# Ordering the residual stream's transposes ahead of other side work in a hybrid decoder step on one Trainium2 core

## The chip, the core and the metric

The kernel runs on one core of a Trainium2 chip. The metric is the time of one execution in device microseconds, taken as the median of several runs. The core's engines work side by side, each through its own list of instructions in a fixed order: TensorE (PE in the profile), VectorE (DVE), ScalarE (ACT), GpSimd (POOL) and SyncE (SP), whose list holds nearly all the DMA transfers. An instruction waits at the head of its engine's list until what it needs is there, and everything behind it on that engine waits too.

## The reference

One decoder layer is computed for two groups of requests that share the weights: a prompt of 1024 tokens, and 8 samples of 8 tokens with 512 past tokens each in a paged cache (1088 tokens in all, model width 1024).

```
h = rmsnorm(x, norm_mix)
q, k, v, qi, ki, wi, bg, cg, xc, ga, gb = split(h @ w_in)      # rotary on q, k, qi, ki
score = sum_heads(wi * relu(qi . ki)); idx = top_k(score, 256)  # per query, causal
o_a = softmax(q . k[idx]) @ v[idx]
conv_o, conv_new = short_conv(cg * xc, conv_prev, conv_w)       # width 3
x = x + (sigmoid(ga) * o_a + sigmoid(gb) * bg * conv_o) @ w_out
x = x + (silu(g) * u) @ w_down                                  # g, u from rmsnorm(x)
x = x + (p @ w_ple) * sigmoid(rmsnorm(x) @ w_ple_gate)
y = rmsnorm(x, norm_final)
```

The results are y for both groups, the new keys, values and indexer keys, and the last two inputs of the convolution. Everything is in float32; a product is made as three matmuls of a high and a low part of each operand (hi*hi, lo*hi, hi*lo).

## The kernel before, in words

All activations are kept transposed: 128 features on the partitions, tokens along the free axis. The tokens are worked in three chunks of 384, 384 and 320 (`CH`). The input projection is a main line of work: `run_group` makes, for one block of 128 output features and one chunk, 24 matmuls of line 191 (`pj<-h_..,w..`, 8 slices of the width times three products), and goes on to the next chunk and block. The weights come as `wraw`; ACT rounds them to `wh` and POOL subtracts to get `wl` (line 151).

Everything else hangs beside that line as a side stream, a Python generator that emits a few instructions and then says what it needs next: `phase_a` (loads x, normalises it, transposes it to h, chunk by chunk), the indexer's scores, a search of the top 256 by counting on DVE, attention, and so on. The class `Weaver` decides while the program is built whose instructions come next. It keeps a clock of its own for each engine from fixed costs; at each step it takes the first side stream, in the order of its list, whose next instruction would be ready for TensorE now, else the main line, else whatever will be ready first (lines 270 to 310). What it decides is the order in the finished program: at run time each engine goes through its list as it stands.

The streams matter here in three ways. First, `x_keep` (lines 792 to 815) makes a transposed copy of the unnormalised x for the later additions: for each of nine tiles of 128 tokens (the last has 64) it loads x again from memory (SP, 512 KB), makes 8 transposes on TensorE (`pt<-ident,x`, line 198, four into each of two banks `pt`), two copies out by ACT (`xT<-pt`) and one store by SP to the scratch `x_scr`. The tile `xT` comes from a ring called L2, and a load of the next tile of x goes into SP's list behind the store of the one before. The ring `pt` has two banks, shared with `phase_a`, the rotary code's transposes (`pt<-ident,rt`) and attention. Second, `state_in` loads the convolution's state (`sraw`) and makes 8 small transposes of it. Third, the searches run on DVE and attention runs behind them: it needs the outcome of the searches for its masks, and uses TensorE (`at`, `po`), DVE (`mx`, `ptl`) and ACT in turn.

`main` runs the first group `g_first`, then issues four small loads (`c_tri`, `smask`, `sdelta`, `ptab`), and only then starts the streams `state_in`, `x_keep` and the scores, in that order.

Of the kernel before, what the change touches and what calls it, by code (L numbers as in the profile page):

```python
# [105 lines left out]
class Weaver:  # L106
# [162 lines left out]
    def run(self, main):  # L269
        m = Stream(main)  # L270
        LAG_D = 1.5
        while True:
            while self.active < self.max_active and self.queue:
                s = Stream(self.queue.popleft())
                s.t, s.queued = self.T["pe"], True
                self.active += 1
                self.sides.append(s)
            if m.done and not (self.sides or self.queue or self.pending):
                break
            pe = self.T["pe"]  # L280
            self._flush(pe)
            if m.done and not (self.sides or self.queue or self.pending):
                break
            pick = None
            for s in self.sides:
                if not self._hard(s):
                    continue
                if s.kind == "dve":
                    ok = self.T["dve"] <= pe + LAG_D and self._ready(s) <= pe + LAG_D
                elif s.kind == "soon":  # L290
                    ok = self._ready(s) <= max(pe + 0.2, self.T["dve"])
                else:
                    ok = self._ready(s) <= pe + s.ahead and self.T["dve"] <= pe + s.lag and self.T["act"] <= pe + s.lag
                if ok:
                    pick = s
                    break
            if pick is None and not m.done and self._hard(m) and self._ready(m, 3.0) <= pe + 0.3:
                pick = m
            if pick is None:
                best = min((w for w, _ in self.pending), default=None)  # L300
                for s in self.sides + ([] if m.done else [m]):
                    if self._hard(s):
                        r = self._ready(s, 3.0 if s is m else 0.0)
                        r = max(r, self.T["dve"] - LAG_D) if s.kind == "dve" else r
                        if best is None or r < best:
                            best, pick = r, s
                assert best is not None, "no stream can go on"
                self.log.append((max(pe, best) - pe, pick, m)) if hasattr(self, "log") else None
                self.T["pe"] = max(pe, best)
                if pick is None:  # L310
                    continue
            self._step(pick)
            m.t = 0.0
# [3 lines left out]
def hybrid_decoder_step(ctx, tc, I, O):  # L317
# [340 lines left out]
    def x_rows(i):  # L658
        return x_p[i * P:(i + 1) * P, :] if i < 8 else x_s
# [33 lines left out]
    def phase_a():  # L693
        spot = {i: s_all[:, (i - 5) * DM:(i - 4) * DM] for i in range(5, 9)}
        junk = [tM([P, DM], BF, name="junk_a"), tM([P, DM], BF, name="junk_b")]
        xt, tx = {}, {}

        def fetch(c):
            for i, m in tok_tiles(c):
                xt[i] = spot[i] if i in spot else tp_([P, DM], name="x")  # L700
                tx[i] = W.dma(xt[i][:m], x_rows(i))
        yield {"p": 5}
        fetch(0)
        wts.load()
        wts.load()
        fetch(1)
        load_tabs(64)
        sqrt_table()
        ps = psum("po")
        for _ in range(12):  # L710
            W.mm(ps[:, :384], ones, warm, 384, True, True, f32=True)
        W.give("po")
        ev_s = [Ev() for _ in CH]

        def stats(c):

            tl = tok_tiles(c)
            w = len(tl)
            ss = tpool.tile([P, 16], F32, tag="ss", name="ss", bufs=2)
            nc.vector.memset(ss, 1.0)  # L720
            te = t0 = W.cur.t
            for j, (i, m) in enumerate(tl):
                W.cur.t = max(t0, tx[i])
                yield None
                if j == 1:
                    W.go("dve", 1.2)
                    nc.vector.tensor_tensor_reduce(out=junk[1][:m], in0=xt[i][:m], in1=xt[i][:m], scale=1.0, scalar=0.0,
                                                   op0=OP.mult, op1=OP.add, accum_out=ss[:m, j:j + 1])
                else:
                    W.act(junk[0][:m], xt[i][:m], AF.Square, DM, accum_out=ss[:m, j:j + 1])  # L730
                te = max(te, W.cur.t)
            W.cur.t = te
            yield None
            W.ts(ss[:, 4:4 + w], ss[:, 0:w], 1.0 / DM, EPS, OP.mult, OP.add, w)
            W.act(ss[:, 8:8 + w], ss[:, 4:4 + w], AF.Sqrt, w)
            if c == 0:
                t0 = W.cur.t
                wts.pump(True, 1)
                wts.pump(True, 1)
                W.cur.t = t0  # L740
            yield None
            rsqrt(ss[:, 8:8 + w], ss[:, 4:4 + w], ss[:, 12:12 + w], w)
            t0 = te = W.cur.t
            for j, (i, m) in enumerate(tl):
                W.cur.t = t0
                x, r = xt[i][:m], ss[:m, 8 + j:9 + j]
                if j == 0:
                    W.act(x, x, AF.Copy, DM, scale=r)
                elif j == 1 or c == 0:
                    W.ts(x, x, r, None, OP.mult, None, DM)  # L750
                else:
                    W.go("pool", 0.12 + DM * 0.00105)
                    nc.gpsimd.tensor_scalar(x, x, r, 1.0, op0=OP.mult, op1=OP.mult)
                te = max(te, W.cur.t)
            ev_s[c].t = te

        for _ in stats(0):
            pass
        t0 = W.cur.t
        W._flush(1e9)  # L760
        fetch(2)
        ps = psum("pt")
        W.tr(ps[:, 0:56], gtmp[:56, :], ident[:56, :56])
        W.act(gvec, ps[:, 0:56], AF.Copy, 56)
        W.give("pt")
        W.give("S", 2)
        W.cur.t = t0
        for c, (c0, n) in enumerate(CH):
            tl = tok_tiles(c)
            yield ev_s[c]  # L770
            te = W.cur.t
            th = []
            for k in range(KT):
                W.cur.t = te
                tag = "at" if k % 2 else "pt"
                yield {tag: 1}
                ps = psum(tag)
                for j, (i, m) in enumerate(tl):
                    W.tr(ps[:, j * P:j * P + m], xt[i][:m, k * P:(k + 1) * P], ident[:m, :m])
                hs = H["hi"][:, k, c0:c0 + n]  # L780
                W.act(hs, ps[:, :n], AF.Copy, n, scale=g_mix(k))
                W.stt(H["lo"][:, k, c0:c0 + n], ps[:, :n], g_mix(k), hs.bitcast(F32), OP.mult, OP.subtract, n)
                W.give(tag)
                th.append(W.cur.t)
            W.give("p", sum(1 for i, m in tl if i not in spot))
            ev_h[c].t = max(th[1], th[-1] - 3.5)
            if c + 1 < len(CH):
                W.cur.t = 0.0
                yield from stats(c + 1)
        W.give("M", 2)  # L790

    def x_keep():

        for i in range(9):
            m = P if i < 8 else NS
            yield {"p": 1, "L2": 1}
            x, o = tp_([P, DM], name="x"), L2([P, KT, P], name="xT")
            W.load(x[:m], x_rows(i))
            for hf in range(2):
                yield {"pt": 1}  # L800
                ps = psum("pt")
                for k in range(4):
                    W.tr(ps[:, k * P:k * P + m], x[:m, (4 * hf + k) * P:(4 * hf + k + 1) * P], ident[:m, :m])
                t0 = W.cur.t
                W.act(o[:, 4 * hf:4 * hf + 4, :m], ps.rearrange("p (k t) -> p k t", t=P)[:, :, :m], AF.Copy, 512)
                W.give("pt")
                te, W.cur.t = W.cur.t, t0
            W.give("p")
            W.cur.t = te

            def store(i=i, m=m, o=o):
                W.store(x_scr[:, :, i * P:i * P + m], o[:, :, :m])
                W.give("L2")
            W.later(store)
# [1596 lines left out]
            yield from (run_rows if kind == "rows" else run_pair)(*a)  # L2411
    def main():
        wts.pump()
        yield from run_group(g_first)
        W.dma(tri, I["c_tri"])
        W.dma(smask, I["c_smask"])
        W.dma(sdelta, I["c_sdelta"])
        W.dma(ptab, I["page_table"].rearrange("b n -> (b n)").unsqueeze(0))
        W.spawn(state_in(), front=False)
        W.spawn(x_keep(), front=False)  # L2420
        W.spawn(score_stream([2, 3, 4, 5, 6, 7]), front=False)
        W.spawn(samp_idx(), front=False)
        W.spawn(search([2, 3, 4, 5], "a"), kind="dve", front=False)
# [81 lines left out]
```

## Time and profile before

| | |
|---|---|
| median of three runs | 1964.89 us |
| the runs | 3744.03, 1963.82, 1964.89 us |
| the profiled execution | 1964.83 us, of which the span is 1963.1 us |
| TensorE busy | 1911.7 us, 97% |
| VectorE busy | 1278.8 us, 65% |
| ScalarE / GpSimd busy | 701.7 / 750.5 us |
| mean granted clock of TensorE | 0.992 |

The profile shows one execution. The span runs from its first instruction to its last; the time lies 1.7 us above it. A busy figure is the time in which an engine had an instruction in work. The rest is waiting, and the profile puts each wait down to the last thing that ended it.

### The profile page before, as it was taken

Reading aid. Unit: us, or ns where it says so; the run is one execution under the profiler, and the core shown is the slowest. Engines: PE = TensorE matmul, PEld = TensorE weight load, DVE = VectorE, ACT = ScalarE, POOL = GpSimd, SP = SyncE. Lnnn points to the kernel's source line nnn. Section 1 sums busy time; section 2 is a strip of 40 time slices with the busy share of each in tenths; the row PEclk is TensorE's granted clock in tenths of the full one; section 3 lists DMA queues with packets and bytes.
Section 4 is the critical chain, followed back from the end, with each engine's and each line's share of the span. In section 5 each row is a group of like instructions: output and inputs, shape, how many; then the busy total and the mean of one; then the engine's idle time right before and its main releaser. Section 6 shows DMA issues by size and latency. Waiting matters only on the chain.

```text
span 1963.1 us, 35813 instructions
## 1 busy us (share of the span) xinstructions
PE 1911.7 (97%) x13337; PEld 1852.5 (94%) x13337; DVE 1278.8 (65%) x2691; ACT 701.7 (36%) x1403; POOL 750.5 (38%) x662
## 2 busy tenths in 40 slices
PE   8999989999999999999999899999999999999998
PEld 5998889998999989989999899999999999999998
DVE  6646999999999975214338885665665643314754
ACT  5355433213443235323334542322322322213543
POOL 2543455223322233114444342322322454424883
PEclk9999999999999999999999999999999999999999
DMA  4565335222322222546443432222222443212343
GB/s 154 170 190 151 99 105 145 54 56 66 85 65 52 63 74 54 154 126 198 126 146 121 145 101 76 77 83 70 79 83 66 139 150 99 89 47 85 105 135 118
DMA packets 293688, 206.27 MB, mean 105 GB/s; under 512 B 28912, under 2 KB 273192, under 8 KB 293514
## 3 DMA queue, kind: packets, MB, share of 16 engines
q1 hardware_dynamic: 293190, 203.63, 35.1%
q8 instruction: 105, 1.72, 0.4%
q14 instruction: 69, 0.57, 0.1%
q10 hardware_dynamic: 324, 0.36, 0.1%
HBM read 152.61 MB, written 51.31 MB: 104 GB/s over the span
## 4 chain that ended last, share of the span: by engine, by line
PE 81%; DVE 9%; issue 3%; DMA 3%; POOL 2%; SPq 1%; ACT 0%; DVEq 0%; POOLq 0%; ACTq 0%
PE pj L155 44%; PE pj L191 26%; PE at L187 4%; PE po L187 3%; PE pt L198 3%; DVE junk L1235 2%; SPq L164 1%; DVE ru L136 1%; POOL wl L151 1%; DVE cum L1271 1%; PE at L198 1%; DMA wraw<-in_w_in 1%; DMA qh<-qh_scr 0%; DVE scores L140 0%; DVE cv L140 0%
## 5 line engine op out<-in xcount | busy, mean ns | idle before, releaser
L151 POOL TENSOR_TENSOR wl<-wraw,wh 128x512 fp32r<-128x512 f32 (+2 forms) x234 | 302.4, 1295 | 660.2 <-ACT wh L132 636.5
L191 PE MATMUL pj<-h_hi,wh 128*128 128x384 f32 (+2 forms) x1197 | 404.9, 338 | 0.6 <-DVE ru L136 0.3
L191 PE MATMUL pj<-h_hi,wl 128*128 128x384 f32 (+2 forms) x1197 | 394.0, 329 | 0.7 <-POOL wl L151 0.7
L191 PE MATMUL pj<-h_lo,wh 128*128 128x384 f32 (+2 forms) x1197 | 393.6, 329 | 0.0
L132 ACT ACTIVATE wh<-wraw 128x512 fp32r<-128x512 f32 (+2 forms) x234 | 142.3, 611 | 295.8 <-PE pj L155 136.7
L191 PEld LDWEIGHTS pj<-h_hi,wh 128*128 128x128 f32 (+1 forms) x1197 | 226.4, 189 | 10.7 <-issue 6.3
L191 PEld LDWEIGHTS pj<-h_lo,wh 128*128 128x128 f32 (+1 forms) x1197 | 226.3, 189 | 2.8
L191 PEld LDWEIGHTS pj<-h_hi,wl 128*128 128x128 f32 (+1 forms) x1197 | 225.7, 189 | 1.8 <-POOL wl L151 1.1
L155 PE MATMUL pj<-f_hi,wl 128*128 128x272 f32 x704 | 204.3, 290 | 5.5 <-DVE wl L136 5.5
L155 PE MATMUL pj<-f_hi,whl 128*128 128x272 f32 x1056 | 206.0, 288 | 0.0
L155 PE MATMUL pj<-f_hi,wh 128*128 128x272 f32 x704 | 204.0, 290 | 0.3 <-DVE q_lo L136 0.2
L155 PE MATMUL pj<-f_lo,wh 128*128 128x272 f32 x704 | 203.3, 289 | 0.2 <-DVE f_lo L136 0.2
L136 DVE TENSOR_TENSOR x<-pj,x 128x272 f32<-128x272 f32 (+2 forms) x144 | 67.0, 469 | 173.4 <-PE pj L155 170.0
L155 PE MATMUL pj<-m_hi,wh 128*128 128x272 f32 (+2 forms) x586 | 176.1, 300 | 1.2 <-DVE x L136 0.7
L155 PE MATMUL pj<-m_hi,wl 128*128 128x272 f32 (+2 forms) x586 | 175.7, 300 | 0.0
L155 PE MATMUL pj<-m_lo,wh 128*128 128x272 f32 (+2 forms) x586 | 175.5, 300 | 0.0
L155 PEld LDWEIGHTS pj<-f_hi,whl 128*128 128x128 f32 x1056 | 168.7, 189 | 0.0
L155 PE MATMUL pj<-f_lo,whl 128*128 128x272 f32 x528 | 152.3, 288 | 0.0
L155 PEld LDWEIGHTS pj<-f_hi,wl 128*128 128x128 f32 x704 | 133.6, 190 | 5.9 <-DVE wl L136 5.9
L155 PEld LDWEIGHTS pj<-f_hi,wh 128*128 128x128 f32 x704 | 133.4, 189 | 0.6 <-issue 0.6
L155 PEld LDWEIGHTS pj<-f_lo,wh 128*128 128x128 f32 x704 | 133.3, 189 | 0.4 <-DVE f_lo L136 0.4
L151 POOL TENSOR_TENSOR whl<-wraw,whl 128x512 fp32r<-128x512 f32 x68 | 94.2, 1388 | 74.0 <-ACT whl L132 72.0
(376 smaller groups left out, 4488.1 us busy)
## 6 DMA issues: line engine op xcount, KB each, us to landing
wraw<-in_w_in SPq DMA_DIRECT2D x112, 256.0 KB
wraw<-in_w_gate_up SPq DMA_DIRECT2D x96, 256.0 KB
wraw<-in_w_down SPq DMA_DIRECT2D x40, 256.0 KB
wraw<-in_w_out SPq DMA_DIRECT2D x32, 256.0 KB
wraw<-in_w_ple_gate SPq DMA_DIRECT2D x32, 256.0 KB
x<-in_x_prompt SPq DMA_DIRECT2D x13, 512.0 KB
m_scr<-q_lo SPq DMA_DIRECT2D x19, 272.0 KB
q_lo<-m_scr SPq DMA_DIRECT2D x18, 272.0 KB
```

Of the source, the lines that this page charges most:

```text
L132: self.nc.scalar.activation(out, in_, func, **kw)
L136: self.nc.vector.tensor_tensor(out, a, b, op=op)
L151: self.nc.gpsimd.tensor_tensor(out, a, b, op=op)
L155: self.nc.tensor.matmul(ps, l, r, start=start, stop=stop)
L164: self.nc.sync.dma_start(out, in_)
L187: self.nc.tensor.matmul(ps, l, r, start=start, stop=stop)
L191: self.nc.tensor.matmul(ps, l, r, start=start, stop=stop)
L198: self.nc.tensor.transpose(ps, in_, ident)
L1235: nc.vector.tensor_scalar(junk[:m, :L], score[q], cand[:m, i:i + 1].bitcast(F32), None, op0=op, op1=OP.add, accum_out=cnt[:m, i:i + 1])
L1271: nc.vector.tensor_tensor_scan(cum, eq, eq, 0.0 if last is None else last, op0=OP.add, op1=OP.bypass)
```

## The change

`x_keep` is started ahead of `run_group(g_first)`, so it stands in the list before `state_in` and the scores. It begins once the loads of the last chunk of x have been issued (`ev_x2`). Until `g_first` is through, its transposes are of a kind `fill`: the Weaver takes them only where no side stream and not the main line has an instruction ready. From then on they are of the ordinary kind, and the stream is asked first among those that were started in `main`.

```diff
@@ class Weaver, run @@
             for s in self.sides:
                 if not self._hard(s):
                     continue
+                if s.kind == "fill":
+                    continue
...
                 pick = m
+            if pick is None:
+                pick = next((s for s in self.sides if s.kind == "fill" and self._hard(s) and self._ready(s) <= pe + 0.2), None)
             if pick is None:
                 best = min((w for w, _ in self.pending), default=None)
@@ phase_a @@
         fetch(2)
+        ev_x2.t = W.cur.t
@@ x_keep @@
+    keep, ev_x2 = ["fill"], Ev()
+
     def x_keep():
 
+        yield ev_x2
         for i in range(9):
             m = P if i < 8 else NS
+            W.cur.kind = "pe"
             yield {"p": 1, "L2": 1}
             x, o = tp_([P, DM], name="x"), L2([P, KT, P], name="xT")
             W.load(x[:m], x_rows(i))
+            W.cur.kind = keep[0]
             for hf in range(2):
@@ main @@
         wts.pump()
+        W.spawn(x_keep(), front=False)
         yield from run_group(g_first)
...
         W.spawn(state_in(), front=False)
-        W.spawn(x_keep(), front=False)
+        keep[0] = "pe"
+        for s in W.sides:
+            s.kind = "pe" if s.kind == "fill" else s.kind
         W.spawn(score_stream([2, 3, 4, 5, 6, 7]), front=False)
```

The instructions are the same ones; their order differs. The change moves the nine groups of 8 transposes forward in TensorE's list, from instructions 325 to 938 of some 13,100 to instructions 161 to 724, and it moves the 8 transposes of `sraw` back from 275 to 838. The first place is TensorE at the start of chunk 3's transposes of the normalised x (`scores` is where that chunk's x lies). A piece of the difference:

```order
 L191 MATMUL pj<-h_lox,wh 128x384
 L191 MATMUL pj<-h_hix,wl 128x384
+L198 MATMUL pt<-ident,x 128x128 x8
 L198 MATMUL pt<-ident,scores 128x128 x2
 L198 MATMUL pt<-ident,scores 128x64
```

The first tile of `x_keep` now stands between the last matmul of a chunk and the transposes of the next one. The second tile stands at the end of `g_first`, ahead of the first 128x384 matmul of the next block. The third stands 30 matmuls further: 24, three transposes of `rt`, and 6 more.

The second place is SP at that third tile, in the loads behind `g_first`. Before:

```order
L164 DMA ptab_95<-in_page_table 1x32
L164 DMA sraw_644<-in_state_conv 16x1024
L164 DMA wraw_688<-in_w_in 128x4x128
L164 DMA qi_scr_61<-ru_622 128x256
L164 DMA qi_scr_61<-rt_621 128x256
```

And now:

```order
L164 DMA ptab_95<-in_page_table 1x32
L164 DMA x_scr_67<-xT_526 1024x1x128
L164 DMA x_714<-in_x_prompt 128x1024
L164 DMA wraw_717<-in_w_in 128x4x128
L164 DMA qi_scr_61<-ru_641 128x256
L164 DMA qi_scr_61<-rt_640 128x256
```

The load of the third tile of x, and a load of weights behind it, now stand behind the store of the second tile's `xT`. On ACT the two copies that make this `xT` stand right behind a group of three `wh<-wraw 128x512`, ahead of `ki_hi<-rt 64x256`; no `xT` stood there before.

The third place is TensorE at the end of attention, where the last of its outputs `ob` is transposed (its instruction 5119 before, 5053 now). Before:

```order
L191 MATMUL pj_10323<-h1_lo_98,wh_9941 128x384
L191 MATMUL pj_10323<-h1_hi_96,wl_9942 128x384
L198 MATMUL pt_10359<-ident_85,ob_10351 128x128
L191 MATMUL pj_10323<-h1_hi_96,wh_9966 128x384
L191 MATMUL pj_10323<-h1_lo_98,wh_9966 128x384
```

And now:

```order
L191 MATMUL pj_10220<-h1_lo_98,wh_9872 128x384
L191 MATMUL pj_10220<-h1_hi_96,wl_9873 128x384
L198 MATMUL pt_10272<-ident_85,ob_10264 128x128
L191 MATMUL pj_10220<-h1_hi_96,wh_9872 128x384
L191 MATMUL pj_10220<-h1_lo_98,wh_9872 128x384
```

Of the projection's matmuls of line 191, 612 stood behind that transpose before and 678 do now: 66 more. On DVE, whose list holds the same work ahead of the last of attention's `ptl<-pt,pth` but for one instruction, nothing of that size has moved. Of TensorE's list the first 161 and the last 8,000 or so instructions are in the same order in both.

## Rows read from the trace of the kernel before

**Rows 1.** The page's head and its busy times (engine, us, share, instructions).

```profile
span 1963.1 us, 35813 instructions
PE 1911.7 (97%) x13337; PEld 1852.5 (94%) x13337; DVE 1278.8 (65%) x2691; ACT 701.7 (36%) x1403; POOL 750.5 (38%) x662
```

**Rows 2.** Windows by stage: stretch, length, busy time (count) of each engine, clock, DMA.

```profile
0.00:195.00 195.00, 182.81 (x1050) 158.98 (x1051) 116.84 (x216) 96.38 (x210) 78.88 (x80) 0.96 0.57 167
195.00:700.00 505.00, 488.58 (x3012) 471.08 (x3010) 479.83 (x1201) 164.89 (x355) 180.48 (x194) 0.99 0.28 78
```

**Rows 3.** Timeline around 44 us: start, duration, engine, instruction, [idle before, releaser].

```profile
43.63 1.15 ACT L132 ACTIVATE scores<-scores,ss 128x1024 f32<-128x1024 f32 x1 [1.04 <-DVE ss L136]
44.83 0.86 PE L198 MATMUL pt<-ident,scores 128*128 128x128 f32 x3 [1.65 <-ACT scores L132]
```

**Rows 4.** Timeline of 61 to 82 us, all engines.

```profile
64.75 0.63 ACT L132 ACTIVATE wh<-wraw 128x512 fp32r<-128x512 f32 x1 [3.76 <-DMA wraw<-in_w_in]
66.08 0.47 SPq L164 DMA_DIRECT2D ptab<-in_page_table  x1
66.55 0.33 PE L191 MATMUL pj<-h_hi,wh 128*128 128x384 f32 x1
67.04 0.39 SPq L164 DMA_DIRECT2D wraw<-in_w_in  x1
68.64 0.67 PE L198 MATMUL pt<-ident,sraw 16*128 16x16 f32 x8 [0.89 <-DMA sraw<-in_state_conv]
73.14 0.42 SPq L164 DMA_DIRECT2D x<-in_x_prompt  x1
73.23 0.63 ACT L132 ACTIVATE wh<-wraw 128x512 fp32r<-128x512 f32 x1 [1.43 <-PE pj L191]
77.27 1.06 PE L198 MATMUL pt<-ident,x 128*128 128x128 f32 x8 [1.09 <-DMA x<-in_x_prompt]
78.09 0.42 PE L191 MATMUL pj<-h_hi,wh 128*128 128x384 f32 x1
77.93 1.09 ACT L132 ACTIVATE xT<-pt 128x512 f32<-128x512 f32 x2 [2.25 <-PE pt L198]
79.04 0.57 SPq L164 DMA_DIRECT2D x_scr<-xT  x1
79.67 1.80 SPq L164 DMA_DIRECT2D x<-in_x_prompt  x1
```

**Rows 5.** Windows around chunk 3's transposes, and at 77 us (columns as in Rows 2).

```profile
46.10:51.70 5.60, 5.60 (x19) 2.87 (x19) 4.59 (x9) 4.45 (x10) 1.81 (x3) 0.50 0.00 0
51.80:56.20 4.40, 4.40 (x20) 3.94 (x20) 2.46 (x5) 1.49 (x4) 0.81 (x2) 0.50 0.27 93
56.40:61.00 4.60, 4.60 (x33) 4.57 (x32) 1.73 (x5) 1.81 (x4) 1.05 (x2) 1.00 0.34 78
77.20:82.00 4.80, 4.73 (x30) 4.76 (x31) 0.86 (x2) 1.92 (x4) 2.74 (x4) 1.00 0.85 237
```

**Rows 6.** Timeline at 1128 us, TensorE.

```profile
1127.78 0.40 PE L155 MATMUL pj<-f_hi,wl 128*128 128x272 f32 x1 [4.34 <-DVE wl L136]
```

**Rows 7.** Windows behind that wait (columns as in Rows 2).

```profile
1128.00:1131.50 3.50, 3.50 (x17) 3.50 (x17) 3.46 (x6) 2.13 (x5) 1.42 (x1) 0.51 0.24 66
1131.50:1135.00 3.50, 3.50 (x30) 3.50 (x29) 2.48 (x6) 1.29 (x3) 0.03 (x1) 1.00 0.30 88
```

**Rows 8.** Waits of DVE in 195 to 700 us.

```profile
DVE u L136 <- PE pj L191: 3.0, 3, 2.2
DVE cv L136 <- PE pj L191: 2.1, 3, 1.3
DVE p L1304 <- PE at L187: 1.2, 3, 0.7
DVE rt L136 <- PE pj L191: 1.1, 1, 1.1
```

## The prediction

> **What bounds the kernel now.** I read the page's busy times first. TensorE is busy 1911.7 of 1963.1 us [rows 1], so the kernel can gain little by moving work: all of TensorE's waits together are 1963.1 - 1911.7 = 51 us, and a change that only reorders can take some of them away or add to them. Next come the windows by stage [rows 2]. In the first 195 us TensorE is busy 182.81 us, and the reader should see that DVE has slack there (116.84 us). Between 195 and 700 us that is gone: DVE is busy 479.83 of 505 us beside TensorE's 488.58. In this stretch two engines are near full, and either may set the pace. Then the timeline, for the three waits that lie where the change works. TensorE stands still for 1.65 us ahead of chunk 3's transposes, until ACT has scaled x [rows 3]; for 0.89 us until `sraw` has landed, and for 1.09 us until the first tile of x for `x_keep` has landed [rows 4]. Last come the granted clock in windows of a few us [rows 5, 7]: it tells what a wait costs beyond its own length.
>
> **The change, part by part.** No instruction is added, so every term is a wait or the clock.
>
> *First tile.* Its 8 transposes go into the 1.65 us wait. Eight take 0.82 us (from 77.27 to the next matmul at 78.09 [rows 4]). But they take both banks `pt`, and chunk 3's first transposes need one back. The copies out stand on ACT behind the scaling, which ends at 43.63 + 1.15 = 44.78 [rows 3]; two copies take 1.09 us [rows 4], so the first bank is free at about 45.33 instead of the start at 44.83. The wait shrinks by 0.82 and grows by 0.50: **-0.32 us**. The ends: -0.82 if the bank costs nothing, +0.3 if chunk 3's own copies, now behind both of these on ACT, are late throughout.
>
> *The two other waits.* The wait for `sraw` goes, since its transposes come over 500 instructions later and its load is then long landed: **-0.89**. The wait of 1.09 goes, since the first tile's load now stands on SP right behind chunk 3's own, which ACT is scaling by then: **-1.09**.
>
> *Third tile.* Here a new wait appears, and this is the step I trust most. The ring L2 gives out one tile at a time at this point, so the third load stands on SP behind the second tile's store, and that behind ACT's two copies. On ACT the copies stand behind the third `wh`, which itself waits for its weights and runs from 64.75 to 65.38; two copies more end at 66.47. SP is through with `ptab` at 66.55, the store takes 0.57, so the load is issued at 67.12. From issue to the first transpose a tile took 77.27 - 73.14 = 4.13 us: 71.25. TensorE gets there after six matmuls of a new chunk, where the seventh started at 66.55 before, and now 0.50 later for the first tile and 0.82 for the second: 67.87. All of this is [rows 4]. The wait is 71.25 - 67.87 = **+3.4 us**. The ends are 1.1 (the wait that the same load left before) and 5.5 (issued over 1.80 us, as the row at 79.67, and landing as much later). Behind that load on SP is a load of weights, moved back from 67.04 by some 2 us; what it feeds starts at 73.23 and waited for TensorE, not for it [rows 4], so I cost this at nothing; without that cover it is at most those 2 us. From the fourth tile on, 50 instructions and more lie between two tiles, so I expect no such wait again.
>
> *The clock.* [...] After the wait of 1.09 us with 8 transposes the clock stayed at 1.00 (77.20 to 82.00 in [rows 5]). [...]
>
> *Attention.* Since the transposes and the scores come earlier, the planner put less of the projection ahead of attention: the last transpose of its outputs has 66 fewer of line 191's matmuls ahead and 66 more behind, up to 66 x 0.167 = 11.0 us (at full clock 33 of the 320-token chunk start in 4.60 us [rows 5], 0.139 each, so 0.167 for a chunk of 384). DVE's work ahead of the same point is unchanged. If DVE sets the pace up to there, its end does not move and TensorE has 11.0 us more to do afterwards. But DVE itself waited 3.0 + 2.1 + 1.2 + 1.1 = 7.4 us for TensorE [rows 8], and with TensorE sooner at those points the waits can go: 11.0 - 7.4 = **+3.6**. The ends are 0, if TensorE sets the pace, and 11.0. No row shows which of these holds; I take the middle, since both engines were over 95% busy.
>
> The sum: -0.32 - 0.89 - 1.09 + 3.4 + 1.5 + 3.6 = +6.2. The profiled execution took 1964.83 us, 0.06 from the median of 1964.89, so the forecast is **1971 us**.
>
> **The rivals.**
>
> *A plain gain.* The third load is on time or its wait is covered, the clock is not touched, and attention keeps its pace: -0.32 - 0.89 - 1.09 = -2.3, or 1962.5 us. For it: each of the three waits is plainly there, and 67.87 depends on costs that I moved by hand. Against it: the chain of ACT, SP and a load of 4.13 us leaves no way to 67.87. Chance 0.26.
>
> *The clock is held.* At 46 us the clock fell to 0.50 and stayed there for some 10 us, through 19 transposes and 20 matmuls [rows 5]. If the fill keeps it from falling, the 20 matmuls would take 20 x 4.60 / 33 = 2.8 us instead of 4.4, and the transposes, then held by DVE's 4.59 busy us, 1.0 less: 2.6 more gained, 1960 us. Against it: what fills the wait is transposes alone, and in the windows the engine was busy for all of 5.60 us with transposes alone, at 0.50, and rose to 1.00 only after 4.4 us of matmuls [rows 5]. Chance 0.07. [...]
>
> *Slower by DVE.* DVE sets the pace from 195 to 700 us and its own waits do not go away, since they come at points where TensorE isn't earlier. Then the whole 11.0 us count: 7.4 above the forecast, 1978.4 us. It decides from the point at which attention's waits for `mx` and `ptl` grow by more than DVE's fall. For it: 479.83 of 505 us busy [rows 2]. Against it: DVE had 25 us not busy there, and of them 7.4 waiting for TensorE. Chance 0.21.
>
> *Nothing moves.* The new wait eats the old ones and attention absorbs the rest: 1964 to 1967 us. Chance 0.06.
>
> **How the numbers follow.** The forecast, within 1967 and 1975, has the chance 0.40. From 1960, where the plain gain and half of the clock's rival still lie, to 1979, where DVE's rival ends, about 0.8 is held; below and above I leave 0.08 and 0.12. No case reaches 2%, which is 39 us and about what a measurement of this kernel can tell from no change; the sum of all ends on the slow side is below 20 us. So within 2%: 0.97; faster 0.01 and slower 0.02 are for what the profile does not show.
>
> **What would show it.** The third tile: a wait of 3 to 4 us of TensorE for x near 68 us, with the load on SP right behind a store of `xT`, and a stretch of 3.5 us at 0.5 behind it. The first: the wait at 43 us cut to some 1.3 us in two parts, and no wait for `sraw` near 68 us. Attention: the sum of TensorE's waits for `mx` and `ptl` up by 3 to 4 us, and DVE's for `pj` down. It would be wrong if the load of the third tile were issued ahead of the store, or if attention ended early by as much as TensorE's moved work.

## The result, and the profile after

The changed kernel takes **1977.28 us** (median of 4 runs, 1975.06 to 1980.04) against 1964.36 us for the kernel before beside it. The ratio is 1.0068, with a 95% interval of 1.0056 to 1.0080: slower by about 13 us, within 2%. One execution of the kernel before, 3744.03 us, lies far outside all others and is not in the ratio. The profiled execution took 1977.82 us, with a span of 1975.9 us against 1963.1. TensorE was busy 1914.8 us and not busy for 61.1 us, 9.7 more than before (in both, 7.4 of that lie behind its last instruction). The 3.1 us of more busy time are the same 13337 instructions at a lower mean clock, 0.988 for 0.992. So the question is where 9.7 us of waits came from.

In the wait ahead of chunk 3's transposes, the timeline of the changed kernel around 44 us (start, duration, instruction, idle before and what ended it) answers to [rows 3]:

```profile
43.08 1.15 ACT L132 ACTIVATE scores<-scores,ss 128x1024 f32<-128x1024 f32 x1 [1.04 <-DVE ss L136]
...
44.26 1.09 ACT L132 ACTIVATE xT<-pt 128x512 f32<-128x512 f32 x2
...
44.91 0.64 PE L198 MATMUL pt<-ident,scores 128*128 128x128 f32 x3 [1.30 <-ACT xT L132]
```

The wait is 1.30 us instead of 1.65, and its releaser has changed: the copy out of the first tile, not the scaling. Counted from the end of the scaling, the transposes start 0.68 us later (44.23 to 44.91) where it was 0.05 (44.78 to 44.83). At the third tile, the timeline of the changed kernel answers to [rows 4]:

```profile
64.76 0.63 ACT L132 ACTIVATE wh<-wraw 128x512 fp32r<-128x512 f32 x1 [3.87 <-DMA wraw<-in_w_in]
...
65.42 1.09 ACT L132 ACTIVATE xT<-pt 128x512 f32<-128x512 f32 x2
...
66.57 0.56 SPq L164 DMA_DIRECT2D x_scr<-xT  x1
...
67.23 0.61 SPq L164 DMA_DIRECT2D x<-in_x_prompt  x1
...
73.16 1.94 PE L198 MATMUL pt<-ident,x 128*128 128x128 f32 x8 [5.53 <-DMA x<-in_x_prompt]
...
74.75 0.67 PE L191 MATMUL pj<-h_hi,wh 128*128 128x384 f32 x1
```

Read it from the top: the third `wh` waits for its weights, the copies out stand behind it, the store behind them, the load behind the store, and TensorE waits 5.53 us for the load. The load took 73.16 - 67.23 = 5.93 us, not 4.13. The windows behind it (columns as in [rows 2]) show the clock:

```profile
70.10:76.70 6.60, 3.54 (x14) 3.57 (x15) 1.01 (x4) 2.12 (x5) 1.23 (x2) 0.50 0.80 233
76.90:83.50 6.60, 6.60 (x44) 6.60 (x43) 3.64 (x7) 1.26 (x2) 1.61 (x2) 1.00 0.71 201
```

The clock of 0.50 lasts 6.6 us and more. The eight transposes in it took 74.75 - 73.16 = 1.59 us instead of 0.82. TensorE works in only the last 3.7 us of that stretch, so it loses about 1.8 us there, an estimate: 0.8 for the eight transposes, and 1.0 for the six matmuls behind them, which took 2.07 us (74.75 to 76.82) where the next ones took 0.17 us each.

The longest added waits lie elsewhere. Two windows of the kernel before, from 195 to 345 and from 345 to 720 us:

```profile
195.00:345.00 150.00, 140.37 (x819) 130.80 (x818) 143.93 (x337) 54.65 (x123) 75.80 (x77) 0.98 0.40 114
345.00:720.00 375.00, 367.38 (x2316) 359.04 (x2316) 347.08 (x901) 118.90 (x249) 112.24 (x125) 1.00 0.25 66
```

The same two of the changed kernel:

```profile
195.00:345.00 150.00, 130.93 (x739) 119.42 (x738) 143.56 (x314) 52.59 (x117) 70.77 (x71) 0.97 0.37 108
345.00:720.00 375.00, 369.30 (x2332) 362.29 (x2331) 346.82 (x916) 118.35 (x251) 112.62 (x131) 1.00 0.25 65
```

In the first, TensorE's waits doubled, from 9.6 to 19.1 us, and it started 80 matmuls fewer; in the second they fell by 2. The first is the end of the scores' work and the start of attention. The waits of TensorE there, in the kernel before:

```profile
PE at L187 <- DVE mx L1304: 2.2, 1, 2.2
PE po L187 <- DVE ptl L136: 2.2, 3, 1.5
PE at L187 <- DVE kidxT L145: 2.1, 1, 2.1
PE at L187 <- ACT relu L132: 1.7, 2, 1.3
```

And in the changed kernel, where each of these kinds is longer and a new one stands last:

```profile
PE po L187 <- DVE ptl L136: 5.7, 3, 3.0
PE at L187 <- ACT relu L132: 3.3, 3, 2.2
PE at L187 <- DVE kidxT L145: 3.3, 3, 2.0
PE at L187 <- DVE mx L1314: 3.1, 2, 3.0
PE at L187 <- ACT wh L132: 2.8, 1, 2.8
```

One of them, followed through the changed kernel's timeline on VectorE and TensorE: a step of attention waits from 290.96 us for `mx`, the maximum of an earlier one.

```profile
286.55 0.61 DVE L1245 TENSOR_SCALAR_CACHE_REDUCE junk<-scores,canda 128x384 uint8<-128x384 f32 x1
...
288.92 1.01 DVE L1245 TENSOR_SCALAR_CACHE_REDUCE junk<-scores,canda 128x768 uint8<-128x768 f32 x1
...
290.35 0.56 DVE L136 TENSOR_TENSOR rt<-pj,cos 128x384 f32<-128x384 f32 x1
...
292.58 0.99 DVE L136 TENSOR_TENSOR ru<-pj,sin 64x320 f32<-64x320 f32 x2
293.60 0.29 DVE L1314 CUSTOM_DVE_ANT_0 p<-at,b 128x128 f32<-128x128 f32 x1
...
293.95 0.33 PE L187 MATMUL at<-k_hi,qh 128*128 128x128 f32 x1 [2.99 <-DVE mx L1314]
```

VectorE is not idle: in its list a whole round of the search and the rotary work of two blocks stand ahead of the first `p,mx`. The wait is one of order.

The balance of the 13 us between the profiled executions, by TensorE's waits in stretches of the trace: 0 to 100 us 13.4 after 10.9 before (+2.5); 100 to 195 us 2.4 after 1.2 (+1.2); 195 to 345 us 19.1 after 9.6 (**+9.4**); 345 to 720 us 5.7 after 7.6 (-1.9); from 720 us to its last instruction 13.1 after 14.4 (-1.3); and the busy time +3.1. Unrounded the sum is +12.9, as is the difference of the spans. Ahead of 195 us the waits thus grew by 3.6, behind it by 6.2.

### The profile page after: what moved, and what is told of

The parts are those of the page before. It is cut to its first block, busy times and chain, and to the rows that moved or that the text cites. A ratio compares the mean times of both kernels' runs of the same rounds, so it can differ in the third digit from the quotient of the medians.

```text
span 1975.9 us, 35789 instructions
## 1 busy us (share of the span) xinstructions
PE 1914.8 (97%) x13337; PEld 1855.6 (94%) x13337; DVE 1276.5 (65%) x2691; ACT 701.4 (35%) x1403; POOL 748.4 (38%) x662
```

## The experiments

Twelve kernels ran, each timed beside the kernel before on the same chip; a ratio is to that. Two theories led the first four: P, that VectorE paces the work up to the end of attention and what counts is how much of the projection is left behind it; E, that the early wait is the cause.

**The late order alone.** One constant of the planner is changed in the kernel before, which leaves TensorE's first 1032 instructions as they were:

```diff
-        self.T["pe"] = s + 0.109
+        self.T["pe"] = s + 0.11
```

> The kernel before with one planner cost changed (a transpose counted as 0.110 us for 0.109). TensorE's first 1032 instructions stand as in the kernel before, x_keep's first eight tiles included; only what follows is ordered otherwise, and 720 of the projection's matmuls stand behind the last transpose of attention's outputs instead of 612. Theory P (the end of attention is paced by VectorE, and what is left behind it costs 0.165 us a matmul): that transpose comes at the same time, near 869 us, and the 108 matmuls add up to 17.8 us: 1976 to 1983 us. Rival E (the changed kernel is slower for its early wait of 5.5 us and the clock behind it): nothing early has changed, so 1963 to 1967 us.

Measured: ratio 1.0045 (1.0029 to 1.0060), 1972.67 us. E expected no loss and is wrong: without any early change 8 us are lost. P expected 11 to 18 more and is wrong in size, and in its reason: it had the last output transpose at the same time, and that came 7.7 us sooner (861.1 for 868.8). The windows show the loss where the changed kernel has it:

```profile
195.00:345.00 150.00, 131.15 (x742) 122.38 (x741) 139.60 (x319) 51.61 (x112) 73.58 (x73) 0.93 0.37 109
```

TensorE waited 18.9 us in it; one wait for `mx` alone was 8.1 us:

```profile
PE at L187 <- DVE mx L1304: 8.1, 1, 8.1
PE at L187 <- DMA qh<-qh_scr: 3.5, 1, 3.5
```

**The load asked for ahead of the buffer**, in the changed kernel, so that the planner issues it earlier:

```diff
-            yield {"p": 1, "L2": 1}
-            x, o = tp_([P, DM], name="x"), L2([P, KT, P], name="xT")
+            yield {"p": 1}
+            x = tp_([P, DM], name="x")
             W.load(x[:m], x_rows(i))
+            yield {"L2": 1}
+            o = L2([P, KT, P], name="xT")
```

> The changed kernel with the load of a tile of x asked for ahead of the buffer for its transposed copy, so that no load waits behind the store of the tile before. 684 matmuls behind the last output transpose (678 in the changed kernel, 612 before). Both theories: the wait of 5.5 us at 68 us goes, and with it the low clock from 70 to 76.8 us. Theory P: VectorE starts some 7 us sooner than in the changed kernel, but 72 matmuls more than before remain, 11.9 us: 1972 to 1977 us. Rival E: 1977.3 less 5.5 and about 3 for the clock, and the filled waits are kept: 1963 to 1968 us.

Measured: 1.0059 (1.0039 to 1.0078), 1977.43 us, just above P's range. The wait for x went, but another took its place, since the planner now put the transposes of `sraw` there and its load stands behind those of x:

```profile
PE pt L198 <- DMA sraw<-in_state_conv: 4.6, 1, 4.6
```

So this run says little on E. The same with the planner's transpose at 0.108 us:

> As the kernel with the load ahead, and a transpose counted by the planner as 0.108 us for 0.109: the first 758 instructions of TensorE stand as there, and 612 matmuls stand behind the last output transpose, as in the kernel before. Theory P: the filled waits are kept and nothing is left behind: 1960 to 1965 us, about 12 below the run with 684. Rival E: the same time as the run with 684, within 2 us.

Measured: 1.0063 (1.0046 to 1.0080), 1977.55 us. Here P falls: 72 matmuls fewer behind attention than in the run before, and the same time, as E had it. And with the side streams asked 0.1 us ahead:

> As the kernel with the load ahead, and a side stream is asked 0.1 us ahead of TensorE's planned time instead of 0.2. 486 matmuls stand behind the last output transpose, 126 fewer than before. Theory P: if VectorE's work still ends as early, up to 126 x 0.165 = 20.8 us less, but TensorE had only 16 us of waits in that stage, and attention now starts 90 instructions later: 1948 to 1962 us. Rival E: 1962 to 1967 us, as nothing early differs.

Measured: 1.0043 (1.0029 to 1.0057), 1972.72 us, slower than both theories' ranges. Between 195 and 345 us TensorE waited 19.0, 14.7 and 10.7 us in these three. Each order that the planner makes anew has other waits, and none of the four was as good as the one before.

**The changed kernel with its loads earlier.** Only SP's list differs from the changed kernel's; each load of x is issued one tile sooner:

```diff
-            W.load(x[:m], x_rows(i))
+            for a in (i, i + 1):
+                if a < 9 and a not in xs:
+                    xs[a] = tpool.tile([P, DM], F32, tag="p", name="x", bufs=8)
+                    nc.sync.dma_start(xs[a][:P if a < 8 else NS], x_rows(a))
```

> The changed kernel with each load of x for x_keep issued one tile earlier on SP; the lists of TensorE, VectorE, ScalarE and GpSimd are instruction for instruction those of the changed kernel. The wait of 5.5 us for the third tile goes, and with it the stretch of 6.8 us at the low clock (3 us). Theory R (the order of what comes after 160 us costs some 7 us, whatever the start): 1977.3 less 6 to 9: 1968 to 1971 us. Rival A (VectorE absorbs an early delay, so an early gain is lost again by the end of attention): 1974 to 1977 us. Rival E (the early wait is all of it): 1963 to 1966 us.

Measured: 1.0064 (1.0047 to 1.0081), 1974.86 us, from 1971.09 to 1978.78. Against the changed kernel's 1.0068 that is no difference that the intervals can tell. The time is in rival A's range, but it cannot decide between the three, since all of them had the wait at the third tile gone. It became 3.52 us, with another releaser, which the timeline of this run shows:

```profile
63.35 0.38 PE L203 MATMUL pt<-ident,rt 72*128 72x72 f32 x3 [0.22 <-ACT xT L132]
...
64.66 0.60 PE L203 MATMUL pt<-ident,x 128*128 128x128 f32 x4
...
68.57 0.16 DVE L145 TENSOR_SCALAR wi_c<-pt 64x8 f32<-64x8 f32 x1 [0.29 <-ACT kio L132]
...
68.78 0.66 PE L203 MATMUL pt<-ident,x 128*128 128x128 f32 x4 [3.52 <-DVE wi_c L145]
```

Four transposes run, then the second four wait for a bank: one of the two `pt` still holds the transposes of `rt`, until VectorE has read `wi_c` from it at 68.57, behind its rotary work. Load and bank each hold the third tile, to within 2 us of each other.

**All else as in the kernel before.** In the next four kernels the planner goes through its plan of the kernel before, and the tiles of `x_keep` named in a list are only counted there; their real instructions are emitted at a given place of TensorE's list. The copy is written over the tile of x, so no buffer of L2 is needed. Every other instruction of every engine keeps its order.

```diff
+            if plan_only:
+                W.take("p"), W.take("L2")
+                W.load_cost(P * DM if i < 8 else NS * DM)
...
+            while W.npe < n_tr or len(W.ring["pt"]) < 2:
+                yield
+            for hf in range(2):
+                ps = PS["pool"].tile([P, 512], F32, tag="pt", name="pt", bufs=2)
```

The first tile alone in the wait at 43 us:

> The kernel before with the first tile alone moved into the wait ahead of chunk 3's transposes; the planner goes through its plan of the kernel before, so every other instruction stands where it stood there. The copy out is written over the tile of x instead of into a buffer of L2. All theories that take the first step of the prediction for right: 1.65 falls to 1.3, the wait for sraw by 0.5, the wait of 1.09 goes: 1.9 us less, 1962 to 1964 us. If moving the transposes forward by itself upsets the scores' stage: above 1966 us.

Measured: 0.9990 (0.9980 to 1.0001), 1962.24 us against 1963.70: 1.5 us less, in the expected range, though the interval just reaches no change. Its profiled execution doesn't show the expected reason. The wait at chunk 3's transposes is not 1.3 us but 2.85, the wait for `sraw` is 0.93, and the second tile now waits 1.3 us for its load:

```profile
45.72 0.64 PE L216 MATMUL pt<-ident,scores 128*128 128x128 f32 x3 [2.85 <-ACT x L839]
67.88 0.67 PE L216 MATMUL pt<-ident,sraw 16*128 16x16 f32 x8 [0.93 <-DMA sraw<-in_state_conv]
```

What fell is TensorE's busy time, 1909.0 us for 1911.7, at a mean clock of 0.993 for 0.992. From 24 to 36 us, where TensorE has the same list in both kernels, the windows of the kernel before and of this run are:

```profile
24.00:36.00 12.00, 9.74 (x54) 8.21 (x53) 10.21 (x20) 6.63 (x13) 5.43 (x5) 0.86 0.28 78
24.00:36.00 12.00, 9.74 (x64) 8.25 (x63) 10.21 (x19) 6.79 (x13) 5.70 (x5) 1.00 0.31 92
```

So TensorE came to chunk 3 sooner and waited longer there: the length of that wait depends on the execution. What does not is the start from the end of the scaling, 0.67 to 0.68 us in all eleven traces with a tile ahead, and 0.05 in the three without. A gain of the first tile by itself is not shown.

All nine at the changed kernel's places, with each load behind the store:

> The kernel before with all nine tiles at the changed kernel's places, each load behind the store of the tile before, and every other instruction in the order of the kernel before (sraw's transposes too). The early wait for the third tile stays (5 us, and about 3 for the clock), the waits for sraw and for the first x go. Theory R (the other order of the later work costs the rest): 1964.8 + 4 to 7 = 1969 to 1972 us. Rival S (what costs is that the transposes are no longer there as filler in the scores' stage, or that this stage starts late): as the changed kernel, 1975 to 1979 us.

Measured: 1.0051 (1.0035 to 1.0068), 1974.02 us, between the two ranges. That is 10.3 us more than the kernel before, with all else in its order, and the interval overlaps with the changed kernel's. With the loads one tile earlier:

> As the run with all tiles moved and the rest as before, with each load issued one tile earlier, so that no tile waits for its load. Theory R: 2 us less than the kernel before, 1961 to 1965 us. Rival S, in its part on the filler: 1968 to 1972 us.

Measured: 1.0041 (1.0026 to 1.0055), 1971.72 us, as the rival on the filler had it: moving the tiles costs 8 us even with no load late. But the windows of this run show that they are lost elsewhere than in the changed kernel:

```profile
195.00:345.00 150.00, 140.77 (x803) 130.88 (x802) 142.53 (x327) 56.38 (x123) 76.24 (x77) 0.95 0.38 111
345.00:720.00 375.00, 365.10 (x2306) 356.89 (x2305) 348.27 (x905) 117.57 (x250) 110.22 (x125) 1.00 0.24 64
```

Between 195 and 345 us TensorE is as busy as in the kernel before, 140.77 us, and waits 9.2 us; with the loads late it is 9.7. So the 9.4 us that the changed kernel waits more in that stretch come with the planner's new order of everything else, not from where the tiles stand. But that does not make them the price of the new order in the time of the whole kernel: with the tiles moved and the old order kept the loss is 10.3 us, with the new order 12.9. In the profiled execution of this run the loss is +1.8 us of waits before 100 us (3.7 for the bank, as above, less the waits that went), +0.5 to 195 us, +2.3 from 345 to 720 us, -0.6 elsewhere, and +2.8 of busy time at a mean clock of 0.989 for 0.992. With the loads late the waits are +6.1 ahead of 195 us and the busy time +3.4, at 0.987.

At this point I had a new theory, V: in all ten traces VectorE took 595 to 604 us from the first addition of a score to the end of its second search, so perhaps it sets the pace there. Three runs tried it. The tiles behind the scores' start:

> The other way round: the first tile in the wait ahead of chunk 3's transposes, and the eight others moved back, behind the start of the scores' work on VectorE (instructions 530 to 1246 of TensorE instead of 375 to 1038); every other instruction in the order of the kernel before. In all runs so far VectorE took 595 to 604 us from the first addition of a score to the end of its second search, and in the runs with this order 596.7 to 598.8, so where it starts should set the end. Theory V (that start is what counts): three tiles fewer ahead of it, 2.5 us, and the waits at 43 and 77 us shortened by 1.4: it starts 3 to 5 us sooner, and the kernel takes 3 to 5 us less than before: 1959 to 1961.5 us. Rival T (TensorE's own work and waits are the sum, and transposes that go into the scores' stage make it longer): 1962 to 1965 us.

Measured: 1.0004 (0.9995 to 1.0014), 1965.03 us, no gain. VectorE did start 5.0 us sooner, at 100.5 us, and then took 604.8 us to the same point instead of 596.7: what TensorE has to do in that stretch counts as well. V is wrong in its main point. Then 10.9 us less of VectorE's work:

```diff
-            counts(OP.is_ge)
+            counts(OP.is_ge, 2 if nm == "a" and b < 9 else 1)
```

> The kernel before, all lists in the same order, with the counts of the last nine rounds of the first search taken over half their columns: 1152 columns less a round at 1.05 ns, 10.9 us less of VectorE's work between 370 and 438 us (the search's result is not the reference's for it). Theory V: VectorE reaches the end of its second search 8 to 11 us sooner and the kernel takes 1954 to 1958 us, less only where TensorE's 16 us of waits in that stage run out. Rival T (TensorE sets the pace, 97% busy): within 2 us of before, 1962 to 1965 us.

Measured: 0.9989 (0.9980 to 0.9998), 1962.61 us, as Rival T had it. Of 10.9 us less, 2.4 arrive. VectorE's own waits show the rest, from 360 to 700 us, where they were 2.8 + 2.1 + 1.2 = 6.1 us in the kernel before:

```profile
DVE cv L136 <- PE pj L191: 6.2, 5, 3.6
DVE u L136 <- PE pj L191: 4.6, 4, 2.2
DVE p L1305 <- PE at L187: 2.5, 3, 1.5
```

It waits for TensorE instead. So behind 345 us TensorE sets the pace, and the same holds in the changed kernel:

> The changed kernel, all lists in the same order, with the same 10.9 us of VectorE's work taken out of the first search (the counts of its last nine rounds over half their columns). Theory V: 1966 to 1970 us, the difference to the kernel before with the same cut about as large as without (11 to 14 us). Rival T: 1975 to 1978 us.

Measured: 1.0059 (1.0041 to 1.0077), 1975.53 us: Rival T. But this cut lies behind the waits that have grown. The last run puts it on them, nine rounds between 265 and 348 us (`17 < b < 27`):

> The changed kernel, all lists in the same order, with the same 10.9 us of VectorE's work taken out of nine earlier rounds of the first search, which lie between 265 and 348 us, where attention's first steps wait (the search's result is not the reference's for it). Theory L (VectorE is late at those steps alone, and TensorE sets the pace elsewhere): the waits for mx and ptl between 285 and 345 us, 8.9 us in the changed kernel, fall by half or more, and the time to 1968 to 1974 us, below the run with the later cut (1975.5). Rival O (those waits come from what stands ahead on TensorE's and ScalarE's lists, whatever VectorE has to do): 1975 to 1978 us, waits as in the changed kernel.

Measured: 1.0030 (1.0018 to 1.0042), 1969.52 us. The same 10.9 us, taken out 100 us sooner, leave a loss of 5.6 us against the kernel before beside it, where the later cut left 10.5 and the changed kernel lost 12.9: they give back 7.3 us instead of 2.4, and the time is in the range of theory L. The intervals of the two cuts just touch. The waits in its profiled execution (which at 1973.48 us is the slowest of its six) bear L out only in part:

```profile
PE at L187 <- DVE mx L1315: 4.6, 1, 4.6
...
PE po L187 <- DVE ptl L136: 3.1, 2, 2.6
...
PE at L187 <- ACT wh L132: 1.9, 1, 1.9
```

`mx` and `ptl` together fell from 8.8 to 7.7 us, not by half, and all of TensorE's waits from 195 to 345 us from 19.1 to 16.5. VectorE's lateness in this stretch costs time, then; through which of these waits is not settled.

## Why the prediction was right or wrong

The forecast was 1971 us, from 1960 to 1979, within 2%. The time lies inside, and the sign is right. But the sum gave +6.2 us where the time rose by 12.9, and what carries the range up to 1979 is a rival whose reason the runs refute. That the number held is luck. Step by step:

*First tile*, -0.32: right in its mechanism, the bank `pt`, and near in size. The start behind the scaling moved by 0.63 us where 0.50 were expected, so 0.82 of work less 0.63 are a gain of 0.19. That the wait itself became 1.30 as forecast is in part chance, since in the run with this tile alone it was 2.85.

*The waits for `sraw` and for the first x*, -1.98: right; neither is left in the changed kernel.

*Third tile*, +3.4: the chain was right to a quarter of a microsecond as far as the load's issue (67.23 for 67.12) and TensorE's arrival (67.63 for 67.87); the last link, the load, took 5.93 us for 4.13, so the wait was 5.53, at the slow end that was given. I also left out the bank held by the transposes of `rt`, which by itself kept TensorE 3.5 us in the run with earlier loads. That no later tile would wait was near enough: 0.56 us at 103 us.

*The clock*, +1.5: no run shows the term for a wait of 3.4 us with 8 transposes behind it. It was my estimate from the wait of 4.34 us in [rows 6] and the matmuls in [rows 7], 13 x 3.5 / 30. What the changed kernel showed in its place, near in size, is a wait of 5.53 us and a clock of 0.50 for 6.8 us (70.0 to 76.8), of which TensorE worked 3.7, so that by the estimate above about 1.8 us were lost. All of TensorE's busy time rose by 3.1; the rest is spread over other stretches and was not in the sum.

*Attention*, +3.6: this step failed, in its mechanism. It said that VectorE's work fixes the end of attention, so that 66 matmuls more behind it cost up to 11.0 us less the 7.4 that VectorE waited. The runs showed three things against it. The number left behind does not set the time (612 and 684 gave 1977.5 both). VectorE does not set the pace behind 345 us (10.9 us less work, 2.4 us gained). And the waits that grew are mostly not the ones that it named. TensorE's waits for `mx` and `ptl` from 195 to 720 us, first in the kernel before, then in the changed kernel:

```profile
PE at L187 <- DVE mx L1304: 5.2, 5, 2.2
PE po L187 <- DVE ptl L136: 4.6, 5, 1.5
PE po L187 <- DVE ptl L136: 5.7, 3, 3.0
PE at L187 <- DVE mx L1314: 5.6, 4, 3.0
```

They rose by 1.5 us (by 4.4 up to 345 us, and fell by 2.9 behind it), not by 3 to 4, and VectorE's for TensorE fell from 7.4 to 5.7 us. TensorE waited 7.5 us more in this stretch, 9.4 more up to 345 us and 1.9 less behind it; the 6 us beside `mx` and `ptl` are for `relu`, `kidxT`, `wh` and others, which the sum did not contain. The 9.4 us come with the planner's new order of the scores' last part and attention's first steps, in which TensorE's next instruction stands ahead of what VectorE and ScalarE deliver. Waits of this size appear there without the tiles moved, from one planner constant, and they are absent there when the tiles are moved and the rest is left in its order. I had compared only how much work stood ahead of a few points in either order, and a sum of work does not show a wait.

Those runs do not say, though, that the new order alone made the kernel slower. With the tiles moved and the rest in its order the kernel lost 10.3 us too, of which the sum's terms ahead of attention, +2.6, had foreseen a quarter.

*The rivals.* Slower by VectorE had 1978.4 us, the number nearest to the result, for a reason that the runs refute. The plain gain did not come. The clock did not hold in the profiled execution of the changed kernel (0.50 from 46.2 to 56.2 us as before); it did, at 1.00, in two others with the same list on TensorE (last section).

What stays open: how the 12.9 us divide between the moved tiles and the new order, whose losses do not add up (10.3 us for the tiles with the old order, 7.9 for one new order without them); and why the order before has so few waits. It is one of six orders of the planner that were run, and the other five lost 8 to 13 us; that says it is a good one, not how to find a better.

## What to carry to other kernels

Where a planner fixes the order of 13,000 instructions, a local change is two changes: the one that was meant, and a new draw of everything behind it. Separate them before judging: keep the plan and move only the instructions in question (it lost 10 us for all nine tiles, 8 with their loads early), and move nothing but perturb the plan (it lost 8). Here each half lost time by itself, and the two losses did not add up. And when a transfer or a bank is to be early, follow each resource that the moved step takes up to what releases it: here the store ahead of a load, and a bank whose last reader stood far down VectorE's list.

## What the runs showed of the hardware that I had not expected

TensorE's clock does not follow from its list alone. The run with the earlier loads has instruction for instruction the changed kernel's list on TensorE. So has the run with the later cut in VectorE's work, which differs from the changed kernel only on VectorE and only behind 390 us. In the profiled executions of both, the clock was 1.00 where that of the changed kernel was 0.50. The windows of the run with the earlier loads, and the first of them in the run with the later cut:

```profile
46.20:51.70 5.50, 5.43 (x31) 3.66 (x31) 4.74 (x10) 5.20 (x11) 2.05 (x3) 1.00 0.62 191
51.80:56.20 4.40, 4.36 (x32) 3.90 (x31) 3.72 (x10) 1.21 (x4) 1.48 (x2) 1.00 0.41 117
46.20:51.70 5.50, 5.43 (x31) 3.67 (x31) 4.74 (x10) 5.23 (x11) 2.05 (x3) 1.00 0.64 191
```

Before and into the first of these windows TensorE did transposes alone, in the run with the earlier loads from 45.64 to 50.36 us, behind a wait of 1.45 us. In the changed kernel the same stretch took 19 instructions where this one took 31. From chunk 3's first transposes to the first 128x384 matmul of the next block the changed kernel took 16.85 us (44.91 to 61.76) and this run 13.08 (45.64 to 58.72). So this fall of the clock is worth some 3.8 us, an estimate from the two stretches, more than the 2.3 us that the filled waits were to give, and the same list has it in one execution and not in another. Transposes alone thus went on at 0.50 in the one execution (from 46.2 us, behind a wait of 1.30) and at 1.00 in the other, through 4.7 us of them behind a wait of 1.45; what decides between the two is not shown.
